# A hybrid long-convolution and attention layer: two rows of sums loaded later, residual rows asked for ahead

## The chip, the cores and the metric

The program runs on one core of one Trainium2 chip. The metric is the device time in microseconds of one execution; lower is better. The engines are TensorE (PE, with weight loads listed apart as PEld), VectorE (DVE), ScalarE (ACT), GpSimd (POOL) and SyncE (SP), which here only issues transfers. On ScalarE and GpSimd transfers are issued too.

## What is computed

One layer for 128 context tokens and 512 latent tokens of width 1024, handled together as 640 columns. The input is modulated, projected by one wide matrix, and goes through two branches: a gated long convolution over the tokens (by Fourier transforms written as matmuls) and a windowed attention. Both are gated, projected, mixed by sigmoid gates and projected once more; a residual and a layer norm end it:

```python
h = x * (1 + scale) + shift
(v_h, x1, x0, g_h), (q, k, v, g_a), m = split_projection(h, p["w_in"], ...)
y_h = hyena_long_conv(v_h, x1, x0, h_fwd, h_bwd, p["hyena_d"])   # (conv(u) + u * d) * x0, u = v_h * x1
...
out = merge_branches(y_h, g_h, y_a, g_a, m, p["w_bh"], p["w_ba"], p["w_out"])
x_new = layer_norm(ALPHA * x + gate * out, p["ln_g"], p["ln_b"])
```

## The kernel before

Activations lie channel by partition, 128 channels a tile, 640 columns (two halves of 320). Every fp32 product is made as three passes with a high and a low part of both factors (`wh`, `wl`, `hH`, `hL`). A projection tile is 48 matmuls into two accumulators of the four of tag `mm`; ScalarE or VectorE then reads them.

The stages, in order: the modulation; four quarters of the long convolution (`quarter_head`, `quarter_tail`, `long_conv`, `long_conv_back`) woven with projections; `hand_over`, which is woven with the last quarter's convolution; two gate projections (`first_gates`, with `gate_a`); 21 pairs of projection tiles computed with seven block products instead of eight (`pair_tile`), woven with the attention; the branch projections; the output projection in five token tiles with the layer norm (`out_tile`, `norm_tile`).

Around the first edit. For the block products, sums and differences of the modulated input are made early (`token_sums`) and stored to a DRAM buffer `tok_d`: four names, `SUMS = ("t2", "t3", "t1", "t4")`, each for two channel groups `r` (0 and 1), each a high and a low row. They are loaded back by `load_sums(r, names)`, two rows a name. For `r = 0` the rows come from the pool `yhp` under the tag `yh`, which has nine buffers:

```python
pool, tag, bufs = homes.pop(0) if r else (yhp, "yh", NK + 1)
t = row(pool, tag, f"{name}_{r}{i}", F32R, bufs)
```

For `r = 1` seven of the eight rows go elsewhere (`homes`), the last to `yh` as well. In `hand_over` the same tag holds also, in the order of the text: `x0_6` and `x0_7`, the multipliers of the last quarter (`quarter_tail`); the loaded sums; `yu6` and `yu7`, the convolution's results (`gate_conv` reads `x0_n` at L474 and stores `yu_n` to DRAM from GpSimd, L522); and `mx0`, `mx1`, tanh of two mixing projections (`mix_tile`, ScalarE at L870, stored from ScalarE at L871). `yu6` and `yu7` come ahead of `mx0` there, because the weave uses up the convolution's steps before the mixing projections. A buffer is handed on when its last reader, or its store, is done.

Up to the end of `hand_over` a planner sets the order of each engine from simulated times. Then comes a block under `manual_schedule` for all five engines, in which every queue runs in the order of the text: `first_gates()`, `sums_of_second()` (two accumulating loads on GpSimd), `scratch()` (four copies within the chip's memory, which overwrite parts of `hH` and `hL` once the second gate projection has read them), loads of sums, weights (`load_a`), biases, and the pairs. The first pair uses its operands in the order `("b11", "t2", "t3", "t1", "b21", "t4", "b22")`, twelve matmuls each; the first half of the twelve takes group `r = 0`, the second `r = 1`.

Around the second edit. At the end, `out_tile(t)` accumulates a token tile of 128 x 1024 and `norm_tile(t)` makes `r = gate * out + ALPHA * x` (L1528, L1529), its statistics (L1530), the norm (L1532 to L1547) and the store (L1551, the last tile L1549 and L1544). The last tile is split into columns of 512, 256 and 256. The row `x` of the residual is loaded in `norm_tile(t)` itself, in two buffers. `load_to` issues on SyncE; there these loads are pinned to the order of the text, so that `x` of a tile stands behind the store of the tile before. The planner orders the rest.

Of the kernel before, what the change touches and what calls it, by code (L numbers as in the profile page):

```python
# [9 lines left out]
F32 = mybir.dt.float32  # L10
# [5 lines left out]
D = 1024  # L16
# [29 lines left out]
def tile_hyena_natten_step(ctx: ExitStack, tc: tile.TileContext, a, o):  # L46
    nc = tc.nc
    P = 128
# [13 lines left out]
    def load_to(dst, src):  # L62
        ins = nc.sync.dma_start(dst, src)
        last[:] = [ins]
        if pinned[0]:
            tc.keep_in_program_order(ins)
# [38 lines left out]
    def row(pool, tag, name, dt=F32, bufs=NK + 1, n=NT):  # L105
        return pool.tile([P, NT + 4 if tag == "yh" else NT], dt, tag=tag, bufs=bufs, name=name)[:, :n]
# [38 lines left out]
    def wraw(i):  # L145
        raws[i] = wp.tile([P, 1024], F32, tag="raw", name=f"raw{i}")
        load_to(raws[i][:], a["wall"][i])

    def wtile(i, eng=None, dst=None, width=P):
        if i in early:  # L150
            return early.pop(i)
        if i not in raws:
            wraw(i)
        if dst is None:
            wh = wp.tile([P, 1024], F32R, tag="wh", name=f"wh{i}")
            wl = wp.tile([P, 1024], F32R, tag="wl", bufs=3, name=f"wl{i}")
            dst = [wh[:]], [wl[:]]
        raw, n = raws.pop(i), 1024 // len(dst[0])
        if eng == "dma":
            (wh,), (wl,) = dst  # L160
            nc.scalar.activation(wl, raw[:], AF.Copy, scale=-1.0)  # L161
            nc.gpsimd.dma_start(wl, a["wall"][i], accum_op=ALU.add)  # L162
            nc.scalar.activation(wh, raw[:], AF.Copy)  # L163
        else:
            for j, (wh, wl) in enumerate(zip(*dst)):
                split(wh, wl, raw[:, n * j : n * j + n], eng)
        return [[w[c // n][:, c % n : c % n + width] for c in range(0, 1024, width)] for w in dst]
# [357 lines left out]
    def quarter_tail(q):  # L525
        for i in range(2):
            n = 2 * q + i
            out["x0"][n] = row(yhp, "yh", f"x0_{n}", n=NG + 1)
            yield from conv_tile(16 + n, out["x0"][n])
            gate_conv(n)  # L530
            yield
# [163 lines left out]
    SUMS = ("t2", "t3", "t1", "t4")  # L695
# [48 lines left out]
    def chain(*gens):  # L744
        for g in gens:
            yield from g
# [61 lines left out]
    def queries(j):  # L808
        for hf, p in enumerate((yield from proj(T_Q + j, eng="dma"))):
            q_half(j, hf, p[:, :HALF])  # L810
        yield
# [31 lines left out]
    def keys(j):  # L843
        cached_keys(j)
        for hf, p in enumerate((yield from proj(T_K + j, eng="dma"))):
            k_half(j, hf, p[:, :HALF])
        yield

    def hand_over():
        yield from quarter_tail(3)  # L850
        hwa_stack.close()
        load_sums(0, SUMS[:3])
        out["slots_l"] = left.enter_context(tc.tile_pool(name="slots_l", bufs=1))
        out["slots_q"] = left.enter_context(tc.tile_pool(name="slots_q", bufs=1))
        first_blocks()
        yield from chain(values(0), queries(0), keys(0))
        yield from mix_tile(0)
        last_mix = mix_tile(1)
        yield next(last_mix)
        for i in range(2):  # L860
            wraw(T_GA + i)
        yield from last_mix
        for i in range(2):
            early[T_GA + i] = wtile(T_GA + i, "dma")
        load_a(0)

    def mix_tile(n):
        th = row(yhp, "yh", f"mx{n}")
        for hf, p in enumerate((yield from proj(T_MH + n, eng="dma"))):
            nc.scalar.activation(th[:, CS[hf]], p[:, :HALF], AF.Tanh, scale=0.5)  # L870
        nc.scalar.dma_start(mh_d[n], th[:])  # L871
        yield
# [16 lines left out]
    def load_sums(r, names):  # L889
        for name in names:  # L890
            for i in range(2):
                pool, tag, bufs = homes.pop(0) if r else (yhp, "yh", NK + 1)
                t = row(pool, tag, f"{name}_{r}{i}", F32R, bufs)
                tok[name][i].append(t)
                load_to(f(t), tok_d[4 * SUMS.index(name) + 2 * r + i])
# [19 lines left out]
    def scratch():  # L915
        for t in (hH, hL):
            for k in range(2):
                load_to(f(t[:, k, HALF:]), f(t[:, 2 + k, :HALF]))
        for tag in ("hHp", "hLp"):
            t = hp.tile([P, 2, NT], F32, tag=tag, name=f"spare_{tag}")  # L920
            spare.extend(t[:, k, c] for k in range(2) for c in CS)
# [216 lines left out]
    def load_a(p):  # L1138
        raws["a", p] = wp.tile([P, 1024], F32, tag="raw", name=f"ra{p}")
        load_to(raws["a", p][:], a["wall"][pairs[p][0]])  # L1140
# [12 lines left out]
    def first_blocks():  # L1153
        blocks(0, *(out["slots_q"].tile([P, NT], F32, tag=t, name=f"rb0_{t}")[:, :512] for t in ("q", "ql")))()
# [212 lines left out]
    with tc.manual_schedule(engines=engines):  # L1367
        for _ in first_gates():
            pass
        sums_of_second()  # L1370
        scratch()
        load_sums(1, SUMS[2:3])
        load_a(1)
        load_sums(0, SUMS[3:])
        load_sums(1, SUMS[3:])
        biases[0] = [bias_tile(h) for h in range(2)]
        for j in range(8):
            side, n_main, n_side = attend(j), N_PAIR * len(HEADS[j].split()), N_ATT if j < 7 else N_ATT + 3
            done = taken = 0
            for _ in mains(j):  # L1380
                done += 1
                while done in (14, 20, 27) if j == 0 else taken * n_main < done * n_side:
                    if next(side, StopIteration) is StopIteration:
                        break
                    taken += 1
                    if j == 0:
                        break
            for _ in side:
                drain()
        drain()  # L1390
# [107 lines left out]
    fin = ctx.enter_context(tc.tile_pool(name="fin", bufs=1, side="right"))  # L1498
# [19 lines left out]
        return [x for part in parts for x in part]  # L1518

    def norm_tile(t, ps, last):  # L1520
        x = fin.tile([P, D], F32, tag="x", bufs=2, name=f"x{t}")
        load_to(x[:], a["xB"][t])
        r = fin.tile([P, D], F32, tag="r", bufs=2, name=f"r{t}")
        st6 = fin.tile([P, 3, 6], F32, tag="st6", bufs=2, name=f"st6_{t}")
        g = gbc[:, 0 if t == 0 else 1]
        for i, (src, c, n) in enumerate(ps):
            h = slice(c, c + n)
            nc.vector.tensor_tensor(r[:, h], g[:, h], src, op=ALU.mult)  # L1528
            nc.vector.scalar_tensor_tensor(r[:, h], x[:, h], ALPHA, r[:, h], op0=ALU.mult, op1=ALU.add)  # L1529
            nc.vector.bn_stats(st6[:, i], r[:, h])  # L1530
        mv = fin.tile([P, 5], F32, tag="mv", bufs=2, name=f"mv{t}")
        nc.vector.bn_aggr(mv[:, 0:2], st6[:, : len(ps)])  # L1532
        nc.scalar.activation(mv[:, 2:3], mv[:, 1:2], AF.Sqrt, bias=eps[:])  # L1533
        nc.vector.tensor_scalar_mul(mv[:, 3:4], mv[:, 0:1], -1.0)  # L1534
        ins = nc.vector.reciprocal(mv[:, 2:3], mv[:, 2:3])  # L1535
        cuts = (0, 480, 960) if last else (0, 512, 1024)
        if last:
            h = slice(960, 1024)
            ins = nc.vector.tensor_tensor(mv[:, 4:5], mv[:, 2:3], mv[:, 3:4], op=ALU.mult)
            tc.keep_in_program_order(ins)  # L1540
            nc.scalar.activation(r[:, h], r[:, h], AF.Identity, scale=mv[:, 2:3], bias=mv[:, 4:5])  # L1541
            nc.gpsimd.tensor_tensor(r[:, h], r[:, h], bc[:, 0, h], op=ALU.mult)  # L1542
            nc.gpsimd.tensor_tensor(r[:, h], r[:, h], bc[:, 1, h], op=ALU.add)
            nc.scalar.dma_start(o["y"][t, :, h], r[:, h])  # L1544
        for h in (slice(*cuts[i : i + 2]) for i in range(2)):
            nc.vector.scalar_tensor_tensor(r[:, h], r[:, h], mv[:, 3:4], bc[:, 0, h], op0=ALU.add, op1=ALU.mult)  # L1546
            nc.vector.scalar_tensor_tensor(r[:, h], r[:, h], mv[:, 2:3], bc[:, 1, h], op0=ALU.mult, op1=ALU.add)  # L1547
            if last:
                nc.sync.dma_start(o["y"][t, :, h], r[:, h])  # L1549
        if not last:  # L1550
            nc.sync.dma_start(o["y"][t], r[:])  # L1551

    for i in range(2):
        load_to(bc[:, i], a["rows"][i + 1 : i + 2].to_broadcast([P, D]))
    for t in range(5):
        ps = out_tile(t, ((0, 512), (512, 256), (768, 256)) if t == 4 else ())
        norm_tile(t, ps, t == 4)
# [135 lines left out]
```

## Time and profile before

| | |
|---|---|
| median of 3 runs | 898.42 us (897.86 to 898.72) |
| the profiled execution | 897.27 us, of which the span from first to last instruction is 895.5 us |
| mean granted TensorE clock | 0.993 |
| busy: TensorE, VectorE, ScalarE, GpSimd | 97%, 71%, 50%, 21% of the span |
| HBM traffic | 187 GB/s over the span |
| the 16 transfers `t<-tok_d` | 320 KB each, 5.5 us from issue to landing |
| the 5 transfers `x<-xB` | 512 KB each, 4.3 us |

Times in the profile are us from the start of the span. A line of the timeline is: start, duration, engine (a `q` behind it: only an instruction issued by its sequencer, such as a transfer), line of the kernel, operation, output<-inputs, shapes, count; in brackets the idle time of the engine before it and what ended it. A line of the waits is: who waited, for whom, total us, times, longest. Rows of the slices divide the span into 40 parts of 22.4 us; a digit is a busy share in tenths.

### The profile page before, as it was taken

The page shows a single profiled execution, that of the slowest core. Times are in us where ns is not written, and L with a number is a line of the kernel's source. Part 1 is how long each engine was busy: PE and PEld are TensorE (multiplying, and loading weights), DVE is VectorE, ACT ScalarE, POOL GpSimd, SP SyncE. Part 2 cuts the span into 40 slices and gives each one's busy share as a digit, 9 for nine tenths or more (in the row PEclk, how much of TensorE's full clock was granted, in tenths as well). Part 3 has the DMA queues.
Part 4 walks back from the last instruction along what each step waited for, and adds up shares of the span by engine and source line. Part 5 has one row for each costly group of instructions (what it writes and reads, how often), then busy time and mean ns, then how long its engine had stood idle before and what let it go on. Part 6 is the DMA issues. An engine that isn't in the chain of part 4 may idle for free. (4 is left out here: it accounts for less than half of the span.)

```text
span 895.5 us, 17141 instructions
## 1 busy us (share of the span) xinstructions
PE 870.1 (97%) x6476; PEld 839.2 (94%) x6476; DVE 637.4 (71%) x1215; ACT 450.3 (50%) x956; POOL 190.2 (21%) x216
## 2 busy tenths in 40 slices
PE   8999999999999999799999999999999999999995
PEld 7789999999899999799999999999999999999884
DVE  4897584985687458379877777777877676667566
ACT  4485545654464454267656666666666622233200
POOL 0020101210101111119354335333554200000000
PEclk9999999999999999899999999999999999999998
DMA  8976575877547686698586758665854586445332
GB/s 331 404 208 145 132 160 140 221 185 176 137 100 174 161 234 136 210 301 279 150 249 150 219 154 237 165 193 168 232 133 125 188 322 216 166 164 184 114 103 89
DMA packets 75246, 169.09 MB, mean 189 GB/s; under 512 B 11003, under 2 KB 28667, under 8 KB 75164
## 3 DMA queue, kind: packets, MB, share of 16 engines
q1 hardware_dynamic: 56204, 123.06, 41.5%
q0 software_dynamic: 13632, 39.33, 22.6%
q10 hardware_dynamic: 5328, 5.61, 1.8%
q8 instruction: 51, 0.84, 0.4%
q14 instruction: 31, 0.25, 0.1%
HBM read 143.32 MB, written 23.99 MB: 187 GB/s over the span
## 5 line engine op out<-in xcount | busy, mean ns | idle before, releaser
L1234 PE MATMUL sp<-t,wb 128*128 128x320 f32 x1008 | 158.9, 311 | 0.0
L1234 PEld LDWEIGHTS sp<-t,wb 128*128 128x128 f32 x1008 | 150.1, 188 | 0.5 <-issue 0.5
L1234 PE MATMUL sp<-hH,wb 128*128 128x320 f32 x500 | 121.0, 313 | 0.0
L182 PE MATMUL mm<-hH,wh 128*128 128x320 f32 x336 | 84.1, 316 | 9.6 <-ACT mx L870 4.2
L1234 PEld LDWEIGHTS sp<-hH,wb 128*128 128x128 f32 x500 | 86.1, 188 | 2.6 <-issue 2.6
L182 PE MATMUL mm<-hL,wh 128*128 128x320 f32 x336 | 82.2, 313 | 0.4 <-DVE hL L329 0.4
L182 PE MATMUL mm<-hH,wl 128*128 128x320 f32 x336 | 81.5, 312 | 0.4 <-DVE wl L102 0.4
L1234 PE MATMUL sp<-hL,wb 128*128 128x320 f32 x250 | 77.3, 309 | 0.0
L162 POOL DMA_DIRECT2D wl<-wall x34 | 30.3, 891 | 220.0 <-ACT wl L161 201.1
L182 PEld LDWEIGHTS mm<-hH,wh 128*128 128x128 f32 x336 | 57.6, 190 | 12.0 <-ACT mx L870 4.5
L163 ACT ACTIVATE wh<-raw 128x1024 fp32r<-128x1024 f32 x34 | 36.1, 1063 | 63.0 <-PE mm L182 47.8
L1195 DVE TENSOR_TENSOR wb<-s,wb 128x512 fp32r<-128x512 f32 x63 | 45.0, 716 | 20.3 <-ACT wb L1187 20.2
L182 PEld LDWEIGHTS mm<-hL,wh 128*128 128x128 f32 x336 | 57.7, 190 | 1.5 <-DVE hL L329 1.2
L182 PEld LDWEIGHTS mm<-hH,wl 128*128 128x128 f32 x336 | 57.6, 190 | 1.3 <-DVE wl L102 0.9
L1002 POOL TENSOR_SCALAR edge<-edge,sm 128x320 f32<-128x320 f32 x32 | 43.4, 1514 | 63.7 <-DVE sm L1000 63.7
L1187 ACT ACTIVATE wb<-s 128x512 fp32r<-128x512 f32 x63 | 39.7, 631 | 32.0 <-PE sp L1234 20.3
L1002 POOL TENSOR_SCALAR p<-p,sm 128x384 f32<-128x384 f32 x32 | 50.3, 1670 | 22.3 <-DVE sm L1000 9.4
L1234 PEld LDWEIGHTS sp<-hL,wb 128*128 128x128 f32 x250 | 47.0, 188 | 0.0
L1512 PE MATMUL out<-woh,yhs 128*128 128x512 f32 (+1 forms) x176 | 45.7, 373 | 0.0
L1222 DVE TENSOR_TENSOR spare_hHp<-sp,yu 128x320 f32<-128x320 f32 x63 | 30.5, 483 | 17.0 <-PE sp L1234 10.7
L182 PE MATMUL mm<-yhs,wh 128*128 128x320 f32 x224 | 42.0, 309 | 0.0
L1542 POOL TENSOR_TENSOR r<-r,bc 128x64 f32<-128x64 f32 x1 | 0.3, 321 | 176.7 <-ACT r L1541 176.7
(415 smaller groups left out, 2284.5 us busy)
## 6 DMA issues: line engine op xcount, KB each, us to landing
raw<-wall SPq DMA_DIRECT2D x54, 512.0 KB, 3.8
wl<-wall POOLq DMA_DIRECT2D x34, 512.0 KB, 6.0
ra<-wall SPq DMA_DIRECT2D x21, 512.0 KB, 4.5
rb<-wall SPq DMA_DIRECT2D x40, 256.0 KB, 5.2
ada<-wada SPq DMA_DIRECT2D x16, 512.0 KB, 8.3
tm<-bias SPq DMA_DIRECT2D x16, 512.0 KB, 8.2
s<-wall SPq DMA_DIRECT2D x21, 256.0 KB, 5.2
s<-wall POOLq DMA_DIRECT2D x21, 256.0 KB, 4.5
```

The costliest lines, as they stand in the source:

```text
L162: nc.gpsimd.dma_start(wl, a["wall"][i], accum_op=ALU.add)
L163: nc.scalar.activation(wh, raw[:], AF.Copy)
L182: nc.tensor.matmul(ps[hf][:, :HALF], wt[k], x[:, hf * HALF : (hf + 1) * HALF], start=(i == 0 and k == 0), stop=(i == lead[2] and k == NK - ...
L1002: nc.gpsimd.tensor_scalar_mul(pv, pv, sm[:, 2, c : c + 1])
L1187: nc.scalar.activation(made[g][:, 0], block(g), AF.Copy)
L1195: nc.vector.tensor_tensor(made[g][:, 1], block(g), f(made[g][:, 0]), op=ALU.subtract)
L1222: nc.vector.tensor_tensor(c, dst, c if j == 3 else ps["u"], op=ALU.add)
L1234: nc.tensor.matmul(dst, wk, x(xi, k), start=j < 4 and k == 0 and i == 0, stop=k == 3 and i == 2, skip_group_check=True,)
L1512: ins = nc.tensor.matmul(dst, m[k][:, c0 : c0 + P], w[:, c : c + n], start=(first and k == 0), stop=(last and k == 5), skip_group_check=True,)
L1542: nc.gpsimd.tensor_tensor(r[:, h], r[:, h], bc[:, 0, h], op=ALU.mult)
```

## The change

In `hand_over` the first load of sums takes four rows (`t2`, `t3`) instead of six; the two rows of `t1` for `r = 0` are loaded in the block written in order, behind `scratch()` and ahead of the two for `r = 1`. At the end, the residual rows are held in three buffers: the first three are requested ahead of the tile loop, and each tile requests the row three tiles on, after its statistics and ahead of its store.

```diff
 def hand_over():
     yield from quarter_tail(3)
     hwa_stack.close()
-    load_sums(0, SUMS[:3])
+    load_sums(0, SUMS[:2])
...
     sums_of_second()
     scratch()
+    load_sums(0, SUMS[2:3])
     load_sums(1, SUMS[2:3])
     load_a(1)
     load_sums(0, SUMS[3:])
...
 def norm_tile(t, ps, last):
-    x = fin.tile([P, D], F32, tag="x", bufs=2, name=f"x{t}")
-    load_to(x[:], a["xB"][t])
+    x = xs.pop(0)
...
         nc.vector.bn_stats(st6[:, i], r[:, h])
+    residual(t + 3)
...
 for i in range(2):
     load_to(bc[:, i], a["rows"][i + 1 : i + 2].to_broadcast([P, D]))
+xs = []
+
+def residual(t):
+    if t < 5:
+        xs.append(fin.tile([P, D], F32, tag="x", bufs=3, name=f"x{t}"))
+        load_to(xs[-1][:], a["xB"][t])
+
+for t in range(3):
+    residual(t)
 for t in range(5):
```

## The prediction

> **What bounds the kernel.** I read the page's busy shares and its slices first, then TensorE's waits, then the two places they point at.
>
> ```profile
> PE 870.1 (97%) x6476; PEld 839.2 (94%) x6476; DVE 637.4 (71%) x1215; ACT 450.3 (50%) x956; POOL 190.2 (21%) x216
> PE   8999999999999999799999999999999999999995
> PE mm L182 <- ACT mx L870: 4.2, 1, 4.2
> 760.00:830.00 70.00, 70.00 (x476) 69.74 (x475) 47.01 (x66) 22.93 (x28) 0.00 (x0) 1.00 0.53 174
> ```
>
> TensorE is the bound (97%), so only time in which it waits, runs at a lower clock, or has already ended can be gained. Slice 17 (358 to 381 us) is the one dip inside the program; in it lies TensorE's largest single wait, 4.2 us on the copies `mx`. Behind it the stretches are solid (70.00 of 70.00 us at clock 1.00), so what is gained there arrives at the end. The other place is the last slice, where TensorE is done.
>
> The stretches around the dip (columns: stretch, length, busy us of PE, PEld, DVE, ACT, POOL, then clock, DMA share, GB/s), and TensorE's own order there:
>
> ```profile
> 300.00:322.00 22.00, 22.00 (x180) 21.82 (x179) 15.68 (x28) 12.08 (x21) 2.90 (x4) 1.00 0.71 206
> 354.50:361.70 7.20, 6.10 (x42) 4.85 (x40) 2.94 (x7) 5.58 (x8) 0.00 (x0) 1.00 0.17 34
> 361.70:365.90 4.20, 0.01 (x1) 0.01 (x1) 3.63 (x7) 0.50 (x2) 0.81 (x2) 0.71 0.95 319
> 365.90:370.40 4.50, 4.50 (x17) 4.46 (x18) 0.00 (x0) 0.85 (x3) 2.50 (x7) 0.51 1.06 372
> 359.60 0.28 PE L172 MATMUL yb<-ph,dftL 128*128 128x256 f32 x1
> 360.63 1.04 PE L635 MATMUL y<-pack,ye 128*128 128x128 f32 x8
> 365.89 0.96 PE L182 MATMUL mm<-hH,wh 128*128 128x320 f32 x2 [4.22 <-ACT mx L870]
> 375.06 0.46 PE L182 MATMUL mm<-hH,wh 128*128 128x320 f32 x2
> 382.10 0.31 PE L1234 MATMUL sp<-hH,wb 128*128 128x320 f32 x1
> ```
>
> After the last transposes `y` (end 361.67) TensorE stands 4.22 us, and the first gate projection then runs 4.50 us at clock 0.51.
>
> **Why `mx` is late.** ScalarE and VectorE:
>
> ```profile
> 347.45 1.06 ACT L163 ACTIVATE wh<-raw 128x1024 fp32r<-128x1024 f32 x1 [4.03 <-PE mm L182]
> 354.49 1.06 ACT L163 ACTIVATE wh<-raw 128x1024 fp32r<-128x1024 f32 x1 [3.27 <-PE mm L182]
> 360.32 1.28 ACT L870 ACT_TABLE_LOAD   x1
> 365.40 0.77 ACT L870 ACTIVATE mx<-mm 128x320 f32<-128x320 f32 x2 [3.79 <-DVE yu L474]
> 369.81 0.77 ACT L870 ACTIVATE mx<-mm 128x320 f32<-128x320 f32 x2 [3.65 <-DMA yu_d<-yu]
> 363.63 0.74 DVE L474 TENSOR_TENSOR yu<-x,u 128x64 f32<-128x64 f32 x2
> 364.61 0.75 DVE L474 TENSOR_TENSOR yu<-x,u 128x64 f32<-128x64 f32 x2
> ```
>
> The matmuls of `mx0` and `mx1` were done long before (the weight copies at 347.45 and 354.49 waited for the last of each). What they lack is a row of tag `yh`, of which there are nine: six of sums, `x0_6`, `x0_7`, and one that goes to `yu6`. So `yu7` takes the row of `x0_6` when `yu6` is done, `mx0` that of `x0_7` when `yu7` is done (L474 ends 365.36, `mx0` starts 365.40), `mx1` that of `yu6` when its store has landed (369.81). The order of these rows is the order of the text, not of time. Four accumulators are shared by the projections, two each; `mx0` and `mx1` hold all four, so until `mx0` is out the gate projection has none.
>
> **The change, part by part.**
>
> *Two rows fewer.* Four rows, `x0_6`, `x0_7`, `yu6`, `yu7` and `mx0` are nine: `mx0` waits for no buffer. Its tanh, with the table load 2.05 us, can run on ScalarE any time between its last matmul (347.45) and 361.67. `mx1` is tenth; the first row released is that of `mx0` after its store, or at the latest that of `x0_6` at 364.4. Its accumulators are wanted only by the second gate projection, 7.04 us after the first starts (as the second took, 375.06 to 382.10), so either does. The stall of 4.2 us goes, and with it the slow clock: 4.50 x (1 - 0.51) = 2.2 us. What is late next: nothing that I find for the gate, whose weights are copied by 355.55. But ScalarE now does 0.77 us for `mx1` among the copies on which the transforms before 361.67 depend (TensorE already idles 1.1 us in that stretch). Cost 0 if it goes behind them, 0.8 if ahead; I take 0.4, and as the gain's other end 1.1 us more, should gate products fill those idle gaps. Gain here: 4.2 + 2.2 - 0.4 = 6.0 us, between 5.6 and 7.5. Taking two loads out of the earlier queue is worth nothing there: between 300 and 322 us, where they stand, TensorE is busy 22.00 of 22.00 us.
>
> [...]
>
> *The two rows of `t1`, moved.* Of their two requests the second stood at 315.65. Now they come in SyncE's hand-written order, behind the four copies of `scratch`, which wait for the second gate projection:
>
> ```profile
> 315.65 0.46 SPq L63 DMA_DIRECT2D t<-tok_d  x1
> 376.13 1.34 SPq L63 DMA_DIRECT2D hH<-hHp  x2
> 378.87 1.02 SPq L63 DMA_DIRECT2D t<-tok_d  x2
> 380.47 1.80 SPq L63 DMA_DIRECT2D t<-tok_d  x4
> DMA to landing us min/median/max: 3.3/6.0/7.1
> 383.86 5.47 PE L1234 MATMUL sp<-t,wb 128*128 128x320 f32 x36
> 390.92 1.91 PE L1234 MATMUL sp<-t,wb 128*128 128x320 f32 x12
> 365.66 0.56 POOL L522 DMA_DIRECT2D yu_d<-yu  x1 [0.42 <-DVE yu L474]
> DMA to landing us min/median/max: 5.1/5.2/5.3
> ```
>
> (The first landing line is that of the rows `t` between 355 and 400 us, the second that of `yu`.) On the old clock (the whole group moves up with TensorE) they are issued at 378.87 and 379.4, and everything behind them on SyncE (the other two rows of `t1`, the weights `ra1`, four rows of `t4`, the biases, `ck`) is 1.0 us later. `t1` is the third of the three blocks in the 36 products: it is needed at about 387.4, and its second half 0.9 us on. At the longest landing seen, 7.1 us, the first pair is there by 386.5 and the second by about 387.5 (needed 388.3); `t4`, the first pair by 389.1 (needed 390.92). The margins are 0.8 to 1.8 us, so the cost is 0; if the transfers queue (1.3 MB of `t1` where 0.66 was, at the 372 GB/s above 1.7 us more), up to 1 us at each of two blocks. Their buffers are free: the last user is `yu7`, stored at 365.66 + 5.3 = 371.0, and SyncE comes to `t1` at 378.9 - 6.4 = 372.5.
>
> *Residual rows.* The end of the program:
>
> ```profile
> 873.00:884.40 11.40, 11.38 (x73) 10.10 (x71) 7.94 (x15) 0.29 (x1) 0.00 (x0) 1.00 0.29 101
> 881.34 0.34 SPq L1551 DMA_DIRECT2D y<-r  x1
> 881.73 0.42 SPq L63 DMA_DIRECT2D x<-xB  x1
> 884.41 0.42 DVE L1528 TENSOR_TENSOR r<-gbc,out 128x256 f32<-128x256 f32 x1 [2.41 <-PE out L1512]
> 885.93 1.36 DVE L1529 SCALAR_TENSOR_TENSOR r<-x,r 128x512 f32<-128x512 f32 x3 [1.10 <-DMA x<-xB]
> 887.21 1.34 DVE L1530 BATCH_NORM_STATS2 st<-r 128x6 f32<-128x512 f32 x3
> 888.58 0.23 DVE L1532 BATCH_NORM_AGGREGATE mv<-st 128x2 f32<-128x18 f32 x1
> L1529 DVE SCALAR_TENSOR_TENSOR r<-x,r 128x256 f32<-128x256 f32 x2 | 0.8, 418 | 0.0
> L1530 DVE BATCH_NORM_STATS2 st<-r 128x6 f32<-128x256 f32 x2 | 0.7, 408 | 0.0
> 842.68 1.29 DVE L1529 SCALAR_TENSOR_TENSOR r<-x,r 128x512 f32<-128x512 f32 x2 [1.71 <-DMA x<-xB]
> 848.75 0.34 SPq L1551 DMA_DIRECT2D y<-r  x1
> ```
>
> `x4` is issued only behind the store of tile 3 (881.34) and lands 1.10 us after the last product is there; all three additions and all three statistics of tile 4 then stand in a row. With `x4` asked for in tile 1 (its buffer, that of `x1`, is read out a tile after `x0`, which is at 842.68 to 844) it lies there some 20 us early. Of the last tile's three pieces two are finished before 884.41, and after it come 0.42 (product), 0.42 (addition) and 0.41 (statistics of 256 columns), with 0.04 us between dependent ones: the aggregate starts at 884.41 + 1.34 = 885.75 instead of 888.58, 2.8 us sooner. Its cover is that VectorE is free (7.94 of 11.40 us). If the planner kept the old order (three additions, then three statistics), only the wait of 1.10 would go. Tiles 0 to 3 gain nothing, being under TensorE. What the edit adds at the start, two more loads of 512 KB behind `x0`, could hold `x0` beyond 842.68 by 1 MB, at 372 GB/s 2.8 us; that would move tile 0's store from 848.75 to 851.6, and as VectorE idles 3.5 us even in the last tile (7.94 of 11.40), the later tiles take it in: cost 0.
>
> **Sum.** 4.2 + 2.2 - 0.4 + 2.8 = 8.8 us. The profiled execution took 897.27 us, which gives 888.5; the median of the runs, 898.42, lies 1.15 above it, so I forecast 889.6.
>
> **The rivals.**
>
> *`mx0` waits all the same* (rows counted wrongly, or a row of an earlier tile still held): the dip stays, only the end gains: 898.4 - 2.8 = 895.6. The two releasers of the ScalarE rows fit the count of nine exactly. Chance 0.06.
>
> *`t1` or `t4` lands late*, a new wait in the first pair: up to 2 us back, 891.6. For it: margins under 2 us and full queues. Against it: landings of 6.0 in the middle. Chance 0.08.
>
> *The old order of VectorE at the end*: 1.1 instead of 2.8, 891.3. Against it: two pieces have all inputs well before the third. Chance 0.07.
>
> *The clock falls all the same*: from 359.88 to 361.67 TensorE does nothing but transposes and waiting, 1.8 us, or 2.6 with `mx1`'s copy ahead; if that counts as idle, 2.2 us are lost again: 891.8. [...] The trace has transposes at clock 1.00 in this stretch. Chance 0.04.
>
> *Slower*: SyncE stands at the request for `t1` because its row is not released, and everything behind it in the queue is late with it. It decides if the rows land 8.8 us after the need at 387.4 - 6.4 = 381.0, so, with 6.0 us to landing, if SyncE is held to about 384, 13 us after the last user's store has landed; nothing in the rows holds it so long. Held to 386.5, the time would be about 901. Chance 0.03.
>
> **Numbers.** The forecast has the rest, 0.72, with 887.4 (7.5 here, 3.1 at the end with some overlap of the VectorE pieces, 0.4 of scatter) to 891 as its own range. The range 887.4 to 892.2 takes in the three rivals between 891.3 and 891.8. A measurement of this kernel can tell about 0.2%, 1.8 us: faster 0.95 (all but the slow one and what I may have missed), same 0.02, slower 0.03.
>
> **What would show it.** In the changed profile: no wait of `mm` for `mx`, clock 1.00 from 354 to 382; `mx0` evicted by about 352 with its table load; no wait of `sp` matmuls for `t`; `x4` issued near 847, in tile 1, and on VectorE two of tile 4's statistics ahead of its last product, with under 1.5 us from that product to the aggregate. I would be wrong above all if another wait ends last before the first gate projection, say its accumulators or a ScalarE queue that `mx` now fills.

## The result, and the profile after

The changed kernel took 890.07 us in the median (889.4 to 891.56, 6 runs), the kernel before 897.70 (897.13 to 898.72, 6 runs): ratio 0.9915, 95% interval 0.9902 to 0.9927. The profiled execution took 890.32 us, 6.95 less than that of before. The forecast was 889.6 us, with 8.8 us of gain between the two profiled executions.

The page after, busy shares and TensorE's slices, and, of TensorE's waits, the two between 355 and 400 us that bear on the change (who waited, for whom, total us, times, longest):

```profile
PE 869.3 (98%) x6476; PEld 837.8 (94%) x6476; DVE 637.1 (72%) x1215; ACT 450.3 (51%) x956; POOL 192.9 (22%) x216
PE   8999999999999999999999999999999999999996
```
```profile
PE mm L182 <- ACT mx L870: 0.4, 1, 0.4
PE sp L1234 <- DMA t<-tok_d: 0.4, 1, 0.4
```

The dip of slice 17 is gone, and of the 4.2 us for `mx` 0.4 are left. A wait that was not there before has come: 0.4 us for rows of sums. The stretches around the handover (columns as in the prediction):

```profile
354.50:361.80 7.30, 6.20 (x42) 4.95 (x41) 2.94 (x7) 5.67 (x9) 0.00 (x0) 1.00 0.21 41
361.80:366.00 4.20, 3.80 (x24) 3.65 (x25) 3.58 (x7) 1.45 (x4) 0.89 (x2) 1.00 0.86 275
366.00:372.00 6.00, 6.00 (x43) 6.00 (x42) 1.94 (x4) 1.28 (x3) 2.47 (x7) 1.00 1.06 348
372.00:376.60 4.60, 4.60 (x34) 4.60 (x33) 1.49 (x3) 1.15 (x2) 0.00 (x0) 1.00 0.97 272
```

The clock column is 1.00 throughout, where 0.71 and 0.51 stood. The timeline there, ScalarE and TensorE:

```profile
360.42 1.28 ACT L870 ACT_TABLE_LOAD   x1
361.71 0.77 ACT L870 ACTIVATE mx<-mm 128x320 f32<-128x320 f32 x2
364.75 0.77 ACT L870 ACTIVATE mx<-mm 128x320 f32<-128x320 f32 x2 [2.27 <-DVE yu L474]
362.20 0.75 PE L182 MATMUL mm<-hH,wh 128*128 128x320 f32 x2 [0.44 <-ACT mx L870]
```

`mx0` waits for no buffer any more, but it was not read out by 352 as forecast: the planner put its table load and tanh behind the last copy `yep` of the transforms, so 0.44 us of the wait are left. `mx1` takes the row that the first L474 releases.

The end, on VectorE, and SyncE's loads of `x`:

```profile
877.74 0.69 DVE L1530 BATCH_NORM_STATS2 st<-r 128x6 f32<-128x512 f32 x1
878.34 0.41 DVE L1529 SCALAR_TENSOR_TENSOR r<-x,r 128x256 f32<-128x256 f32 x1
878.78 0.43 DVE L1530 BATCH_NORM_STATS2 st<-r 128x6 f32<-128x256 f32 x1
880.25 0.42 DVE L1528 TENSOR_TENSOR r<-gbc,out 128x256 f32<-128x256 f32 x1 [1.04 <-PE out L1513]
880.70 0.42 DVE L1529 SCALAR_TENSOR_TENSOR r<-x,r 128x256 f32<-128x256 f32 x1
881.16 0.43 DVE L1530 BATCH_NORM_STATS2 st<-r 128x6 f32<-128x256 f32 x1
881.62 0.24 DVE L1533 BATCH_NORM_AGGREGATE mv<-st 128x2 f32<-128x18 f32 x1
```
```profile
830.68 8.99 SPq L63 DMA_DIRECT2D x<-xB  x4
849.06 0.33 SPq L63 DMA_DIRECT2D x<-xB  x1
```
```profile
838.02 1.29 DVE L1529 SCALAR_TENSOR_TENSOR r<-x,r 128x512 f32<-128x512 f32 x2 [1.30 <-DMA x<-xB]
```

Two of the last tile's statistics stand ahead of its last product, and the aggregate follows that product by 1.37 us (4.17 before). `x4` is asked for at 849.06, in tile 1. `x0` is waited for by 1.30 us (1.71 before), so the two loads more behind it cost nothing.

**Where the 6.95 us come from.** Points of the program, from the timelines of the two profiled executions:

| stretch | before, us | after, us | gain |
|---|---|---|---|
| start to the end of the last transposes `y` | 361.67 | 361.77 | -0.10 |
| from there to the first product of the pairs (L1234) | 20.43 | 14.81 | 5.62 |
| to the first product of the output projection | 446.49 | 447.77 | -1.28 |
| to the last product of VectorE with the gate (L1528) | 55.82 | 55.90 | -0.08 |
| to the aggregate | 4.17 | 1.37 | 2.80 |
| to the end of the span | 6.93 | 6.93 | 0 |

So the tail gave what was forecast, the handover 0.4 less, and 1.28 us were lost again in the first pairs. The experiments take these one by one. The end of the last transposes lies up to 6 us apart between the kernels tried (two of them move work in there) and up to 2.6 where their text is the same, so stretches are compared from that point on.

### The profile page after: what moved, and what is told of

Its sections match the earlier page's. It is cut to its first block, busy times and chain, and to the rows that moved or that the text cites. A ratio compares the mean times of both kernels' runs of the same rounds, so it can differ in the third digit from the quotient of the medians.

```text
span 888.5 us, 17140 instructions
## 1 busy us (share of the span) xinstructions
PE 869.3 (98%) x6476; PEld 837.8 (94%) x6476; DVE 637.1 (72%) x1215; ACT 450.3 (51%) x956; POOL 192.9 (22%) x216
## 4 chain that ended last, share of the span: by engine, by line
PE 93%; DVE 4%; ACT 1%; DMA 1%; issue 1%; POOL 0%; SPq 0%; POOLq 0%; DVEq 0%; ACTq 0%
PE mm L182 34%; PE sp L1234 29%; PE out L1513 6%; PE v L656 5%; PE s L1040 2%; PE s L947 2%; PE pt L1031 2%; PE ve L667 1%; DMA t<-tok_d 1%; PE adaT L252 1%; PE yb L171 1%; PE adaT L269 1%; PE yb L172 1%; PE fl L400 1%; PE ut L540 1%
## 5 line engine op out<-in xcount | busy, mean ns | idle before, releaser
L1234 PE MATMUL sp<-t,wb 128*128 128x320 f32 x1008 | 159.5, 311 | 0.4 <-DMA t<-tok_d 0.4
L1234 PEld LDWEIGHTS sp<-t,wb 128*128 128x128 f32 x1008 | 150.3, 188 | 1.3 <-DMA t<-tok_d 0.6
L1234 PE MATMUL sp<-hH,wb 128*128 128x320 f32 x500 | 120.9, 313 | 0.0
L1234 PEld LDWEIGHTS sp<-hH,wb 128*128 128x128 f32 x500 | 86.0, 188 | 2.6 <-issue 2.6
L1234 PE MATMUL sp<-hL,wb 128*128 128x320 f32 x250 | 77.2, 309 | 0.0
L1002 POOL TENSOR_SCALAR p<-p,sm 128x384 f32<-128x384 f32 x32 | 54.1, 1789 | 22.2 <-DVE sm L1000 9.4
L1234 PEld LDWEIGHTS sp<-hL,wb 128*128 128x128 f32 x250 | 47.0, 188 | 0.0
```

The source lines that it names most:

```text
L1002: nc.gpsimd.tensor_scalar_mul(pv, pv, sm[:, 2, c : c + 1])
L1234: nc.tensor.matmul(dst, wk, x(xi, k), start=j < 4 and k == 0 and i == 0, stop=k == 3 and i == 2, skip_group_check=True,)
```

## The experiments

Seven go with the questions whether the two edits add up and what the stall consisted of, four with the 1.28 us. Where a kernel has additional lines, line numbers are shifted by one.

**1. The residual rows alone.** The changed kernel with the loads of sums as before:

```diff
-        load_sums(0, SUMS[:2])
+        load_sums(0, SUMS[:3])
...
-        load_sums(0, SUMS[2:3])
```

> The second edit alone, on the kernel before (six rows of sums early). If the two edits are separate: 2.8 us of gain, all behind the last output product: from its multiplication on VectorE to the aggregate 1.4 us instead of 4.2, the dip with its 4.2 us wait and the clock near 0.5 unchanged; about 894.9 us against 897.7. If the end's gain depended on the first edit (another order of the planner), the three additions would still stand in a row there and only about 1.1 us would go: 896.6.

895.04 us beside 898.52 for the kernel before, ratio 0.9968 (0.9958 to 0.9979). From the last product to the aggregate 1.37 us; from the last transposes to the first pair product 20.42, as before. The tail's gain stands by itself.

**2. The sums alone.** The kernel before with the first edit:

> The first edit alone. If the two edits are separate: 7.6 - 2.8 = 4.8 us or a little less, 893 to 893.6; the first gate projection starts near 362.2, the pairs near 376.6, and the wait of the first pair's products for the rows t, with 0.4 us, is there too, since nothing of the end bears on it. If the t wait came from chance in the transfers, it would differ or be missing here.

894.49 us, ratio 0.9957 (0.9941 to 0.9972). Last transposes to first pair product 14.81. The two edits do not touch each other: 3.48 + 4.03 us by these medians, 7.6 together. In this execution no product waits for `t`, and yet 448.08 us pass from the first pair product to the first output product (446.49 before). Two rows of VectorE, pair 2's sum of weights L1177 and the tail, and TensorE's one wait behind the handover, at the attention scores L947:

```profile
401.66 0.69 DVE L1177 TENSOR_TENSOR s<-s,rb 128x512 f32<-128x512 f32 x1 [1.45 <-issue]
885.17 1.36 DVE L1530 SCALAR_TENSOR_TENSOR r<-x,r 128x512 f32<-128x512 f32 x3 [2.17 <-DMA x<-xB]
PE s L947 <- ACT pts L1026: 1.0, 1, 1.0
```

The first is where the later loss begins and the third where TensorE pays for it (taken up behind experiment 8). The second shows that the wait for `x4` is not always 1.10 us: here it is 2.17, and the stretch from last product to aggregate is 5.25 instead of 4.17.

**3. Five rows of sums instead of four.** The changed kernel, with the first of the two rows of `t1` left where it was:

```diff
         load_sums(0, SUMS[:2])
+        load_sums(0, SUMS[2:3], (0,))
...
-        load_sums(0, SUMS[2:3])
+        load_sums(0, SUMS[2:3], (1,))
```

> Both edits, but five rows early: the high row of t1 is loaded beside the convolution as before, the low one behind scratch. By the count of nine rows (five, x0_6, x0_7, yu6, yu7) mx0 is the tenth and gets the first row to be released, that of x0_6 when yu6's product is done: ScalarE's first mx then starts at about 364.8 instead of 361.7, and the first gate projection at about 365.3: 3.1 us lost. That is an idle time of 3.5 us on TensorE behind the last transposes; whether the clock falls with it is open: 893.2 if it stays 1.00, 895.3 if it falls to 0.5 for 4.5 us. If the wait of mx before came from something other than the number of rows, five rows would cost nothing: 890.

894.24 us, ratio 0.9958 (0.9945 to 0.9971). ScalarE, then TensorE's wait:

```profile
364.57 1.11 ACT L871 ACTIVATE mx<-mm 128x320 f32<-128x320 f32 x3 [2.97 <-DVE yu L474]
```
```profile
PE mm L182 <- ACT mx L871: 3.4, 1, 3.4
```

`mx0` now waits for the first L474, as the count of nine rows says, and comes 0.8 us sooner than before. Yet the pairs start 20.10 us behind the transposes, 0.33 sooner only: the clock falls within a wait of 3.40 us too, and the two gate projections take 16.70 us here against 16.21 before and 14.38 after. Why the shorter wait costs more at the clock is seen when the stretch of half clock is cut out whole, first in the kernel before, then here:

```profile
363.50:370.30 6.80, 4.41 (x16) 4.37 (x17) 1.83 (x6) 1.25 (x4) 3.32 (x8) 0.50 1.03 354
363.75:370.55 6.80, 5.49 (x20) 5.45 (x21) 1.46 (x5) 1.43 (x4) 3.32 (x8) 0.50 1.04 373
```

Both last 6.8 us. TensorE comes back sooner here, so it works through 5.49 us of it where it worked through 4.41 before. One row fewer gains next to nothing there (the rest of this kernel's gain is the tail's); the second takes the wait away and the clock's fall with it.

**4. The stall filled.** The kernel before with 28 products of no use ahead of the first gate projection, so that TensorE has work while it waits:

```diff
+        warm = aux("warm")
+        for _ in range(28):
+            nc.tensor.matmul(warm[:, :HALF], hH[:, 0, :P], hH[:, 1, :HALF], start=True, stop=True, ...)
         for _ in first_gates():
```

> The kernel before, with 28 extra products of 128x320 into a spare accumulator bank ahead of the first gate projection (their result is not used). They need nothing that is late and fill the 4.2 us in which TensorE waits for mx. Theory: the slow clock behind that wait comes from the idle time alone. Then the granted clock stays 1.00, the wait itself ends when it ended (first gate projection about 4.2 us after the last transposes), and the two gate projections take 14.1 us instead of 16.2: 2.1 us faster than before, 896. If the slow stretch had another cause (the transfers of that time, or the transposes), the clock would still read about 0.5 there and the time would not change.

```profile
361.70:366.00 4.30, 4.13 (x30) 3.87 (x28) 3.73 (x7) 0.50 (x2) 0.81 (x2) 1.00 0.98 317
366.00:372.00 6.00, 6.00 (x40) 5.86 (x40) 0.00 (x0) 1.03 (x3) 2.52 (x7) 1.00 1.04 325
```

The gate projection starts as late as before (365.99), but at clock 1.00; the two projections take 14.37 us instead of 16.21. That is the clock's part by itself: 1.84 us. From the first pair product to the first output product nothing is lost (446.50). The whole gains less, 897.11 us beside 898.20, ratio 0.9982 (0.9972 to 0.9991). In the profiled execution 1.48 us of the gain are lost again at the tail (5.65 us from last product to aggregate, 4.17 before); whether the other runs lose as much there is not shown.

**5. The weave stretched in the kernel before.** The weave of `hand_over` with the last convolution gets a larger count, so that the convolution's steps last until after the mixing projections and `mx0` is ahead of `yu6` and `yu7` in the text:

```diff
-    weave(hand_over(), ..., 4 * NK + N_VALUES, N_CONV + N_BACK + 1)
+    weave(hand_over(), ..., 6 * NK + N_VALUES + 7, N_CONV + N_BACK + 1)
```

> The kernel before with all six rows early; only the weave of hand_over with the last convolution is spread (the count of main steps 62 instead of 43), so that mx0 stands ahead of yu6 in the text. Theory: the rows go in the order of the text, so mx0 now takes the ninth row and yu6 waits for its store, which has long landed. Then ScalarE does mx0 right behind its matmuls, near 349, the 4.2 us and the slow clock go, and as t1 is not moved no product waits for t: pairs 14.4 us after the last transposes instead of 20.4, about 6 us faster than before, 892. If the number of rows alone decides, the wait stays and the time is that of before, 898.

```profile
350.56 0.77 ACT L870 ACTIVATE mx<-mm 128x320 f32<-128x320 f32 x2
371.53 0.77 ACT L870 ACTIVATE mx<-mm 128x320 f32<-128x320 f32 x2 [5.07 <-DVE yu L474]
```
```profile
PE mm L182 <- ACT mx L870: 4.2, 1, 4.2
```

With six rows of sums still loaded, `mx0` is out at 350.56: the order of the text alone decides who gets the ninth row. Now `mx1` waits for L474, and TensorE's wait of 4.2 us has moved to the second gate projection; the first runs among the last transforms (355.26 to 365.33), which for that end 6.15 us later. The pairs start at 380.77, where 382.10 stood. 896.30 us, ratio 0.9978 (0.9968 to 0.9988): the stall is as long, with the slow clock behind it (0.66 in the mean of 372.00 to 377.00 us), and moving it gains little.

**6. The same weave in the changed kernel.**

> Both edits, and the weave spread in the same way. mx0 is then done near 349 instead of 361.7 with its table load, so the 0.4 us that TensorE still waits for it goes. The store of mx0 lands before 357, so the request on SyncE that now stands 6.6 us for its landing (the one for the second row of t3) does not stand, the queue reaches scratch with fewer transfers in flight, and the wait for t4 shrinks or goes: up to 1.2 us faster than the changed kernel, 889. If the requests for t4 are late only because of the four of t1 and the full queues, the wait of 0.4 us stays: 889.7.

```profile
PE sp L1234 <- DMA t<-tok_d: 3.8, 4, 1.8
```

896.32 us, ratio 0.9983 (0.9968 to 0.9998): slower than the changed kernel. The stall is gone and the first pair product stands at 374.18, 6.9 us behind the last transposes. But in this text the rows `t` are asked for only from 369.6 us on (360.05 in the changed kernel), the last request for `t4` is done at 382.5, and the products wait four times. Among these waits the clock falls once more: 0.84 in the mean of 374.20 to 396.00 us, where it is 1.00 from 361.00 to 374.20. From the first pair product to the first output product 455.47 us pass, 7.70 more than in the changed kernel: what TensorE gains at the handover, the late rows take back, and more.

**7. Two residual buffers.** The changed kernel with `residual(t + 2)` and two buffers:

```diff
-            xs.append(fin.tile([P, D], F32, tag="x", bufs=3, name=f"x{t}"))
+            xs.append(fin.tile([P, D], F32, tag="x", bufs=2, name=f"x{t}"))
...
-        residual(t + 3)
+        residual(t + 2)
```

> Both edits, but the residual rows in two buffers again, asked for two tiles ahead: x4 is then requested in tile 2, near 860, 20 us before its use. Theory: at the end the place of the request ahead of the store counts, not the third buffer. Then the aggregate comes 1.4 us after the last product as with three buffers, 890. If the third buffer mattered, x4 would land later and part of the 2.8 us would be lost, up to 892.8.

890.77 us, ratio 0.9919 (0.9899 to 0.9939); last product to aggregate 1.37 us. What counts is that `x4` is asked for ahead of a store, not the third buffer.

**8. `t1` ahead of the copies `scratch`.** The changed kernel, SyncE's order alone changed:

```diff
+        load_sums(0, SUMS[2:3])
         sums_of_second()
         scratch()
-        load_sums(0, SUMS[2:3])
```

> Both edits, but the two rows of t1 requested ahead of the four copies of scratch instead of behind them. Theory 1: the rows t4 came late (0.4 us of wait and about as much in the restart) because two requests and 0.66 MB more stand before them behind scratch. Then the wait of sp for t goes and the stretch from the start of the pairs to the first attention scores is 0.8 us shorter (12.4 instead of 13.2): 889.3. Theory 2: they are late because TensorE is 5.5 us ahead and the transfers of the results yu and mx, which are not, now fall into the same time; then the wait stays at 0.3 us or more, 890.1. If t1 ahead of scratch delays scratch itself, the first pair's own post-processing waits instead.

892.00 us, ratio 0.9938 (0.9926 to 0.995). SyncE's timeline and its waits:

```profile
365.40 1.28 SPq L63 DMA_DIRECT2D t<-tok_d  x3
378.62 3.13 SPq L63 DMA_DIRECT2D t<-tok_d  x4
```
```profile
SPq L63 <- DMA mh_d<-mx: 15.7, 1, 15.7
```

The request for `t1` came to stand ahead of rows of other sums and held SyncE for 15.7 us, until the store of `mx0` had landed. `t4` was asked for later than in the changed kernel, and TensorE waited 1.1 us for it. This is the mechanism of the forecast's slower rival, at a small price.

**What stands behind the 1.28 us.** SyncE in the changed kernel, two of its waits between 355 and 392 us, and the landing of the twelve rows `t`:

```profile
362.32 7.34 SPq L63 DMA_DIRECT2D t<-tok_d  x2
370.61 2.66 SPq L63 DMA_DIRECT2D hH<-hHp  x2
373.31 1.45 SPq L63 DMA_DIRECT2D hL<-hLp  x2
374.89 2.19 SPq L63 DMA_DIRECT2D t<-tok_d  x4
377.69 2.97 SPq L63 DMA_DIRECT2D t<-tok_d  x4
384.68 0.33 SPq L63 DMA_DIRECT2D s<-wall  x1
```
```profile
SPq L63 <- DMA mh_d<-mx: 7.0, 2, 6.6
SPq L63 <- DMA t<-tok_d: 2.5, 5, 0.8
```
```profile
DMA to landing us min/median/max: 3.3/6.4/7.4
```

The wait of 6.6 us, for the store of `mx0`, costs nothing: the first copy of `scratch` starts 5.97 us ahead of the first pair product before and after. From there on, SyncE takes longer for the same requests. Of the 3.9 us by which `t4` is asked for later, 1.2 are the two requests more for `t1`; 1.5 are the four copies (4.15 us, 2.63 before) and 1.2 the four requests for `t4` (2.97 us, 1.80 before). Two things are seen. SyncE now stands for landings of earlier rows `t`, up to 0.8 us at a time: the requests at 383.88, 384.68, 385.44 and 386.24 us each start within 0.08 us of the landing of the transfer eight before (383.80, 384.62, 385.42, 386.22). And the requests for `t4` last 0.57 to 0.80 us each, where 0.36 to 0.42 before, although only the first of them stood for such a landing; why is not shown. Before, the transfers had thinned out there, since TensorE's stall had let them land (DMA share 0.62, against 0.97 and above after):

```profile
370.40:382.10 11.70, 11.70 (x82) 11.70 (x82) 3.43 (x6) 2.62 (x6) 0.00 (x0) 1.00 0.62 180
```

So `t4` and, behind it, the biases and pair 2's weights are asked for later behind the first pair product than I reckoned. Two prices follow: the wait of 0.42 us for `t4`, and VectorE's sum of pair 2 (L1177), which needs weights that GpSimd adds up once SyncE's first halves have landed. Before and after, with GpSimd's request and its time to landing after:

```profile
403.61 0.68 DVE L1177 TENSOR_TENSOR s<-s,rb 128x512 f32<-128x512 f32 x1
```
```profile
399.66 0.69 DVE L1177 TENSOR_TENSOR s<-s,rb 128x512 f32<-128x512 f32 x1 [0.44 <-DVE sm L973]
392.34 0.86 POOL L1165 DMA_DIRECT2D s<-wall  x1 [23.69 <-DVE sm L973]
DMA to landing us min/median/max: 7.2/7.2/7.2
```

GpSimd's half lands at 399.58 and L1177 starts at 399.66. The row of L1177 names the softmax (L973) as what ended the idle time, but L973 had been done for 0.44 us. Set side by side with the kernel before, product by product from the first pair product on, the changed kernel is 0.79 us behind ahead of the scores (L947), by the wait for `t4` and what follows from it; it is 1.15 behind from the scores on, and 1.28 at the output.

The executions that bear on it, in us behind the first pair product (worked out from the timelines and the landings of the transfers):

| kernel | `t4` asked for by | TensorE's wait for `t` | pair 2's weights asked for | GpSimd's half lands | L1177 | first output product |
|---|---|---|---|---|---|---|
| before | 0.17 | none | 4.46 | 16.77 | 21.51 | 446.49 |
| weave stretched (5) | 3.91 | none | 7.32 | 22.00 | 22.08 | 446.46 |
| sums alone (2) | 2.84 | none | 6.66 | 22.97 | 23.05 | 448.08 |
| two buffers (7) | 3.02 | none | 7.22 | 22.41 | 22.50 | 447.76 |
| after | 4.08 | 0.42 | 8.10 | 23.00 | 23.08 | 447.77 |
| `t1` ahead of `scratch` (8) | 4.60 | 1.1 | 9.41 | 24.08 | 24.16 | 448.85 |
| `t1` by GpSimd (9) | 2.55 | none | 6.23 | 20.79 | 21.52 | 446.63 |
| weights ahead (10) | 2.05 | none | 4.13 | 17.47 | 23.94 | 448.66 |
| both (11) | 2.80 | none | 4.27 | 16.17 | 22.57 | 447.28 |

In the five executions in which L1177 waits for GpSimd's half, it starts 0.08 to 0.09 us behind that landing, so this is what holds it. A delay of 0.57 us (5) costs TensorE nothing, one of 0.99 (7) costs 1.27. The first column scatters: up to the requests for `t4` the text of the handover is the same in 2, 7, 10 and the changed kernel, and they are done by 2.05 to 4.08. TensorE's wait for `t` came in one of these four, the loss at the scores in all. The last three experiments test this reading.

**9. `t1` requested by GpSimd.**

```diff
         sums_of_second()
+        load_sums(0, SUMS[2:3], nc.gpsimd)
         scratch()
-        load_sums(0, SUMS[2:3])
```

> The changed kernel, but its two rows of t1 for r = 0 are requested by GpSimd, right behind its two accumulating loads, and no longer by SyncE. Theory (SyncE's pace: with eight transfers under way a request stands until an older one has landed, about 0.75 us each): two requests fewer stand ahead of t4, so t4's four are done about 1.5 us sooner, near 2.6 us behind the first pair product instead of 4.08; no product waits for t (0.78 us gained), and the second half of pair 2's weights is added up soon enough that VectorE's sum of L1177, 23.08 us behind the first pair product now, comes at about 21.5 to 21.8. From the end of the last transposes to the first output product 461.4 to 461.8 instead of 462.58; time 889 to 889.4. Rival (it is the volume: the transfer engines were busy 0.99 from 370 to 382 us, and the same bytes are moved): t4 lands no sooner, the wait stays at 0.4 to 0.8, L1177 stays near 23, 462.6, time 890.1. Second rival (GpSimd's request waits for the rows and its transfers are slow, as the 9 us of its accumulating loads are): t1 is late, a wait for t of 1 us or more, time 891 or above.

889.56 us beside 897.94 for the kernel before, ratio 0.9916 (0.9897 to 0.9935). GpSimd, SyncE and VectorE:

```profile
369.69 1.13 POOL L896 DMA_DIRECT2D t<-tok_d  x2 [0.50 <-DMA mh_d<-mx]
376.08 3.12 SPq L63 DMA_DIRECT2D t<-tok_d  x4
382.88 0.33 SPq L63 DMA_DIRECT2D s<-wall  x1
398.18 0.69 DVE L1178 TENSOR_TENSOR s<-s,rb 128x512 f32<-128x512 f32 x1
```

No product waits for `t`, L1177 (L1178 here) does not wait, and TensorE stands at the scores no longer than before. From the last transposes to the first output product 461.43 us pass, in the range that the theory of SyncE's pace gave (461.4 to 461.8); the changed kernel has 462.58 and the other two executions with the same handover (2 and 7) 462.89 and 462.57. The same bytes were moved at a DMA share of 0.9 and more from 367 us on, so it was not the volume alone. As a version it is 1.15 us better in that stretch of the trace; the intervals of the ratios overlap, so the timed runs do not show it faster than the changed kernel.

**10. Pair 2's weights ahead of the biases.** The changed kernel:

```diff
-        biases[0] = [bias_tile(h) for h in range(2)]
...
                 done += 1
+                if done == 9 and j == 0:
+                    biases[0] = [bias_tile(h) for h in range(2)]
```

> The changed kernel, but the two bias tiles of the first two heads (512 KB each) are requested behind the weights of pair 2 instead of ahead of them. Theory (the scores near 407 us are late because pair 2's weights are requested 8.1 us behind the first pair product instead of 4.5, and its second half is added only when they have landed): the requests come at about 6, L1177 does not wait and stands at 21.51 plus what the wait for t4 costs (0.78), and the further 0.37 us at the scores are not lost: 462.2 from the last transposes to the first output product instead of 462.58, time 889.7. The wait for t4 stays, since it is requested before. Rival (the scores are late for another reason, such as TensorE coming early to work that ScalarE paces): L1177 without a wait, but still 1.15 us lost by 410 us. Rival on the other side: the biases come too late for the first scores' softmax (needed 14.5 us behind the first pair product, requested at about 8.5, 7 us to landing: up to 1 us late), and VectorE hands that on: 463 or more.

891.30 us, ratio 0.993 (0.9916 to 0.9945). VectorE's waits between 378 and 412 us:

```profile
DVE edge L973 <- DMA tm<-bias: 2.3, 2, 1.6
```

The rival on the other side: the weights are there by far, but the softmax now waits for the biases, L1177 stands behind it in VectorE's order, and 2.17 us are lost instead of 1.28. It does not say what the weights alone are worth; it shows that VectorE's chain of the first heads has little slack against the biases too.

**11. Both.**

> The changed kernel with both: t1 of r = 0 requested by GpSimd, and the biases behind the weights of pair 2. Theory: the wait for t and the wait of L1177 both gone, L1177 at 21.5, first output product 461.4 us behind the last transposes (before: 466.92, that is 5.5 gained at the handover instead of 4.35); time 888.9. Rival (volume): one of the waits stays, 462.2 or more, time 889.7 or more.

890.90 us, ratio 0.9921 (0.9908 to 0.9934). The wait for `t` and the weights' are gone, the biases still come 0.8 us late, and 0.79 us are lost. The forecast of 461.4 from the transposes to the output was missed by 0.68, for that reason.

## Why the prediction was right, and where not

**The nine rows** were right: four rows of sums let `mx0` go without a buffer, five make it wait for the first L474 (3), and the order of the text decides (5).

**The stall, 4.2:** 3.78 measured. Rival "`mx0` waits all the same" did not come, but the planner put the tanh at the end of its free time, behind the transforms. I had entered -0.4 for `mx1` among the transforms' copies; `mx1` cost nothing and the 0.44 are `mx0`'s. The size fits, the reason was wrong.

**The clock, 2.2:** mis-sized; 1.83 measured (two gate projections 16.21 before, 14.38 after), and 1.84 with the stall filled (4). I multiplied the length of a stretch by what its mean granted clock lacked. The finished work is the better measure: at clock 0.50 two matmuls follow the two before by 0.53 us, where 0.29 at 1.00, so the clock of 0.50 cost at most 0.45 of the time here and not a half. The 4.41 us of work at 0.50 lost 1.83 us; in experiment 3 the 5.49 us lost 2.3 (16.70 - 14.38). The clock fell 1.8 us into the wait, 3.6 us behind the last product that is no transpose (2.1 and 3.9 us in 3). Rival "the clock falls all the same" did not come: 2.2 us of transposes and waiting are left between those products and the gate (359.98 to 362.20), and the clock stayed at 1.00 there. Whether transposes count as idle, as that rival supposed, is not shown.

**The move of `t1`, 0:** the step that failed. "Everything behind them on SyncE is 1.0 us later" took the two requests at the pace of an emptier queue and left out that the queue does not empty when TensorE is 5.6 us ahead (DMA share 0.97 and above, 0.62 before). `t4` was asked for 3.9 us later behind the first pair product, not 1.0 (1.9 to 2.9 in experiments 2, 7 and 10). Rival "`t1` or `t4` lands late, up to 2 us" is what came, at 1.28 us and at two places, of which I named one: the second, pair 2's weights behind the same queue, was not in the list of what stands behind the move. With two requests fewer on SyncE (9) both are gone. The landings of GpSimd's half show the cause of the second; the first, the wait for `t4`, was missing in 2, 7 and 10 too, so it is in part a matter of scatter.

**The tail, 2.8:** 2.80 in the profiled executions, with the order forecast. Four executions without the second edit had 4.17, 5.25, 5.65 and 5.07 us from last product to aggregate, so three of the four had more to gain than the one that I read.

**The sum.** The parts were 1.85 us too large against the trace (8.8 to 6.95), and the median's 1.15 us above the profiled execution, which I carried over, is not there after (890.32 profiled, 890.07 median). The two errors cancel: forecast 889.6, measured 890.07. That the time came out this close is partly luck.

## What to carry to other kernels

Where buffers of one tag are handed on in the order of the text, count the rows from the front: the stall was one row's place in a list, and one row less of change would have gained almost nothing. When a stall goes, look at what used it as slack: the queue that had thinned out behind the wait here (DMA share 0.62) was full without it (0.97 and above), the four requests for `t4` took 2.97 us instead of 1.80 and later ones stood for landings, up to 0.8 us at a time. So list all that stands behind such requests, with the engine orders that hang on each. Size a slowed clock from work finished in the stretch, not from its mean value: here 4.41 us of work at 0.45 make 2.0 us at most, the mean value gave 2.2, and 1.83 were measured.

## What was not expected of the hardware

In these traces the stretches at clock 0.50 did not go by the length of the wait ahead of them. In the kernel before, TensorE waits 4.22 us and the stretch lasts 6.83 (363.48 to 370.31); in experiment 3 it waits 3.40 us, and the stretch lasts 6.8 as well; in experiment 5 it waits 4.19 us, and the mean clock of 0.66 from 372.00 to 377.00 makes an estimated 3.4 us at 0.50. Nor did the price go by the wait: TensorE worked through 4.41 us of the stretch after 4.22 us of waiting and lost 1.83, and through 5.49 after 3.40 and lost 2.3.

Where a stretch begins differs too. The clock falls 1.8 us into the wait in the kernel before and 2.1 in 3; in 5 it is 1.00 for the whole wait (367.80 to 372.00) and lower only behind it. Near 238 us TensorE waits 1.8 us for ScalarE in the kernel before and 1.7 in the changed kernel, and the clock is 1.00 from 225 to 246 us in both.

The last transposes of experiment 1 (364.25) end 2.6 us later than those of the kernel before (361.67), at the same text up to there; why is not shown. This is more than several of the effects told here, so only the stretches behind that point can be compared at this size.
